# Grouping a split tile's wide products: all high halves first, then all low halves

## Chip, cores and metric

The kernel runs on one core of a Trainium2 chip. The metric is the device time of one execution in microseconds (us), the median of several runs. The engines that matter are TensorE (PE, with its weight loads PEld), VectorE (DVE), ScalarE (ACT) and the DMA queue of SyncE (SP).

## What is computed

One layer of a streaming encoder, in float32, for 256 tokens of width 2048:

```
h = modulate(rms_norm(x), shift1, scale1)
x = x + 0.5 * gate1 * (silu(h @ w1) * (h @ w3)) @ w2            # SwiGLU, hidden width 5632
h = modulate(rms_norm(x), shift2, scale2);  u = h @ w_in        # one projection, cut into parts
y_conv = silu(layer_norm(causal_conv31(glu(u_conv)))) @ pw_w
y_ret  = (silu(g) * group_norm(retention(rotary(q), rotary(k), v))) @ w_o
x = x + gate2 * ((sigmoid(gc) * y_conv + sigmoid(gr) * y_ret) @ w_out)
h = modulate(rms_norm(x), shift3, scale3)
x = x + 0.5 * gate3 * (silu(h @ w1b) * (h @ w3b)) @ w2b
out = modulate(rms_norm(x), shift_f, scale_f)
```

The shifts, scales and gates are products of silu(c) with large matrices (`adaT` in the kernel).

## The kernel before

Channels lie on the 128 partitions (P), the 256 tokens (T) on the free axis; 2048 channels are ND = 16 tiles. A float32 product is made out of exact halves. Every operand is split into a high half in the type fp32r and a low half, the difference. The product is then high x high + high x low + low x high, and the product of the low halves is left out.

Weights come in loads of up to 128 x 2048 elements (1 MB) into one of four `raw` tiles, through the one SP queue (`raw_load`, L92). `prep` (L170) splits each load in two: for each half of its blocks ACT copies up to 128 x 1024 elements into a `hi` tile (L180), and DVE subtracts it from `raw` into a `lo` tile (L182). There are five buffers of each (`HI`, `LO`). `prep` returns one pair (hi, lo) of slices for every 128 x 128 block; with 16 blocks in a load, the first eight lie in one hi tile and the last eight in the next. With 14 blocks they are seven and seven.

Two ways of multiplying stand side by side. `mm3` (L190) makes the three products of 256 columns each, one after the other, into one accumulator; `gemm` (L196) calls it for all blocks. `wide` (L201) makes two products per block instead. The block's high half is multiplied with both halves of the activations, which lie side by side as 512 columns, into a whole bank of 512 (L205). The block's low half is then multiplied with the activations' high half, 256 columns, into the second half of the same bank (L207). The two halves of the bank are added later (`total`, or twice in `Stream.add`). Each of these products loads its own 128 x 128 weights first.

`wide` is used for most of the kernel: the hidden tiles and the second matrices of both SwiGLUs (`ffn`, L333), the gates, `w_o`, `w_pw` and `w_out`. In the second matrix of a SwiGLU the 44 hidden tiles come as 28 and 16 (`GROUPS`); the 28 are loaded as twice 14 blocks. `gemm` or `mm3` is used for the start of each sub-layer, for q, k and the convolution's tiles, for the last column tiles of a sub-layer, and inside the retention's heads. There `value` (L520) calls `mm3` with the roles exchanged: slices of h are the stationary operand, and 512 columns of split weights move.

After each load a tick (L145) issues so much other work: loads of `adaT` that DVE reduces (L102), taps of the convolution, norms. The program's order within each engine is written by a planner that simulates a timeline (`schedule_with_timeline_sim=True`).

Of the kernel before, what the change touches and what calls it, by code (L numbers as in the profile page):

```python
# [14 lines left out]
P = 128  # L15
T = 256
# [10 lines left out]
EPS = 1e-6  # L27

S0 = 6                      # pairs of column tiles worked on side by side, with K outermost
SETS = 4                    # sets of such pairs that the first sub-layer begins with,  # L30
KGROUPS = [3, 4, 4, 5]      # in runs of so many tiles of K
PACE = 0.5                  # units of modulation per load of weights, meanwhile
GROUPS = [28, 16]           # hidden tiles between two visits to x
RAW, HI, LO = 4, 5, 5       # buffers of weights: as loaded, high halves, low halves
# units of modulation, and taps of the convolution, per load of weights
ADA_FFN1, ADA_GATES, ADA_OUT, ADA_FFN2 = 0.7, 0.35, 0.65, 0.35
TAPS_HEADS, TAPS_GATES = 3.8, 3.2

# columns of vecs
V_N1, V_NM, V_N2, V_NF = 0, 16, 32, 48  # L40
# [12 lines left out]
def hybrid_layer(ctx, tc, xT, c, vecs, rope, decay, adaT, w13, w13s, w13t, mixs, w2g, w_ab, w_qk, w_v, w_g,  # L53
# [4 lines left out]
    PE = nc.tensor  # L58
# [16 lines left out]
    x = sb(keep, [P, ND, T], "x1", tag="x")  # L75
# [59 lines left out]

    # ---- work that runs beside the products: so much of it after each load of weights
    rate = {"ada": ADA_FFN1, "taps": 0.0}
# [32 lines left out]
    def prep(src, nk, w, ticks=True):  # L170
        """Loads nk blocks of w columns and splits them; block k -> (hi, lo)."""
        n = nk * w
        r = raw_load(src, n)
        hk = (nk + 1) // 2
        got = []
        for k0 in range(0, nk, hk):
            k1 = min(nk, k0 + hk)
            c0, c1 = k0 * w, k1 * w
            hi = wp.tile([P, 1024], F32R, name="hi", tag="hi", bufs=HI)
            A.copy(hi[:, :c1 - c0], r[:, c0:c1])  # L180
            lo = wp.tile([P, 1024], F32R, name="lo", tag="lo", bufs=LO)
            V.tensor_tensor(lo[:, :c1 - c0], r[:, c0:c1], hi[:, :c1 - c0].bitcast(F32), op=ALU.subtract)  # L182
            for k in range(k0, k1):
                b = slice((k - k0) * w, (k - k0 + 1) * w)
                got.append((hi[:, b], lo[:, b]))
        if ticks:
            tick()
        return got

    def mm3(o, st, mv, start, stop, skip=False):  # L190
        """o += st * mv of exact halves (high, low), without the product of the low ones."""
        PE.matmul(o, st[0], mv[0], start=start, stop=False, skip_group_check=skip)  # L192
        PE.matmul(o, st[0], mv[1], start=False, stop=False, skip_group_check=skip)  # L193
        PE.matmul(o, st[1], mv[0], start=False, stop=stop, skip_group_check=skip)  # L194
# [6 lines left out]
    def wide(o, w, mv):  # L201
        """As gemm, in two parts to be added: o[:, :T] and o[:, T:]; the high half of w stays for both of mv's."""
        n = len(w)
        for k in range(n):
            PE.matmul(o, w[k][0], mv[k].rearrange("p a t -> p (a t)"), start=k == 0, stop=False,  # L205
                      skip_group_check=True)
            PE.matmul(o[:, T:], w[k][1], mv[k][:, 0], start=False, stop=k == n - 1, skip_group_check=True)  # L207

    def product(whole, o, w, mv):
        """gemm where the result is waited for, wide elsewhere."""  # L210
        if whole:
            gemm(o[:, 0:T], w, mv)
        else:
            wide(o, w, mv)

    def total(t, ps):
        """The sums of two column tiles' parts."""
        A.copy(t, ps[:, :, T:])
        V.tensor_tensor(t, ps[:, :, 0:T], t, op=ALU.add)
        return t  # L220
# [6 lines left out]
    def table(f):  # L227
        """Has the table of f in place before it is waited for."""
        A.activation(idle, eps, f)

    def rstd_from(sums, n, name):
        """1/sqrt(sums/n + EPS) by the table, then one Newton step."""
        y = sb(keep, [P, T], name + "_y", tag="rs_y")
        w = sb(keep, [P, T], name + "_w", tag="rs_w")
        r = sb(keep, [P, T], name + "_r", tag="rs_r")
        A.activation(y, sums, AF.Abs_reciprocal_sqrt, bias=eps[:, 0:1], scale=1.0 / n)  # L236
        V.tensor_scalar(w, sums, -0.5 / n, -0.5 * EPS, op0=ALU.mult, op1=ALU.add)
        V.tensor_tensor(w, w, y, op=ALU.mult)
        V.tensor_tensor(w, w, y, op=ALU.mult)
        V.scalar_tensor_tensor(out=r, in0=w, scalar=1.5, in1=y, op0=ALU.add, op1=ALU.mult)  # L240
        return r

    def partition_sums(parts, name):
        """The sum of the parts over tiles and partitions, on all partitions."""
        ps = banks2(name)
        for i, p in enumerate(parts):
            PE.matmul(ps[:, 0, 0:T], ones, p, start=i == 0, stop=i == len(parts) - 1)  # L247
        return ps[:, 0, 0:T]
# [7 lines left out]
    def squares(pool, t, tag="sq", bufs=1):  # L256
        """Adds the squares of two tiles of x to ssq."""
        if t == 0:
            A.activation(ssq, x[:, 0:2], AF.Square)
        else:  # L260
            sq = sb(pool, [P, 2, T], "sq", tag=tag, bufs=bufs)
            A.activation(sq, x[:, t:t + 2], AF.Square)
            V.tensor_tensor(ssq, ssq, sq, op=ALU.add)  # L263

    class Stream:
        """x as a sub-layer's tiles come in: x += gate * y, and the sums of its squares."""

# [22 lines left out]
    def modulated(pool, dst, t, r, n, j, between=None, spare="s"):  # L290
        """Tile t of x * r * scale + shift, split into dst."""
        a = sb(pool, [P, T], "xr", tag="g", bufs=2)
        V.tensor_tensor(a, x[:, t], r, op=ALU.mult)
        if between:
            between()
        if t < 2:
            A.activation(dst[:, t, 0], a, AF.Identity, bias=mod[:, j, t:t + 1], scale=scale[:, n, t:t + 1])  # L297
            f = sb(pool, [P, T], "hf", tag=spare, bufs=2 if spare == "s" else 1)
            V.tensor_scalar(f, a, scale[:, n, t:t + 1], mod[:, j, t:t + 1], op0=ALU.mult, op1=ALU.add)
            V.tensor_tensor(dst[:, t, 1], f, dst[:, t, 0].bitcast(F32), op=ALU.subtract)  # L300
            return
        A.activation(a, a, AF.Identity, bias=mod[:, j, t:t + 1], scale=scale[:, n, t:t + 1])
        A.copy(dst[:, t, 0], a)
        V.tensor_tensor(dst[:, t, 1], a, dst[:, t, 0].bitcast(F32), op=ALU.subtract)
# [12 lines left out]
    def side_by_side(srcs, h, ks, banks, ticks=True):  # L317
        """2 * S0 column tiles at once, a tile of K at a time: products begin with the first of h."""
        for i, k in enumerate(ks):
            w = prep(srcs[k], 2 * S0, P, ticks)  # L320
            across(w, h[k], banks, i == 0, i == len(ks) - 1)

    # ---- a SwiGLU's hidden tile, and its half step
    def hidden(pool, s):
        """From the two projections, in s: the activation's product, split."""
        A.activation(s[:, 0], s[:, 0], AF.Silu)
# [6 lines left out]
    def ffn(pool, i, h, s, store):  # L333
        """s: hidden tiles there already."""
        f0 = 0
# [28 lines left out]

    # ---- first half step: products begin as soon as the first tile of its modulated input is there
    with tc.tile_pool(name="ffn1", bufs=1) as pool:
# [50 lines left out]

    # ---- mixer
    with tc.tile_pool(name="mix", bufs=1) as pool:
# [27 lines left out]
        def normal(dst, n, name, done):  # L447
            """dst = (dst - mean) / std over its n tiles' channels, a few loads apart; then done()."""
            a = sb(pool, [P, 2, T], name + "_a", tag="cs_a", bufs=1)
# [27 lines left out]
        def conv_out():  # L477
            """Swish of the convolution's normed output, split."""
            rate["ada"] = ADA_OUT
# [12 lines left out]
        with tc.tile_pool(name="mix1", bufs=1) as p1:  # L492
# [27 lines left out]
            def value(hd):  # L520
                """v, tokens on partitions."""
                ps = banks2("ps")
# [15 lines left out]
            def scores(hd, qk):  # L538
                """Decayed scores, keys on partitions."""
                (q_hi, q_lo), (k_hi, k_lo) = qk  # L540
# [58 lines left out]
        with tc.tile_pool(name="mix2", bufs=1) as p2:  # L599
# [4 lines left out]
            def gate(src, t, ps=None):  # L604
                """Two tiles of a gate's projection."""
                if ps is None:
# [69 lines left out]

    # ---- second half step, and the final norm
    with tc.tile_pool(name="ffn2", bufs=1) as pool:
# [25 lines left out]
def _blocks(w):  # L704
    """[K, N] -> [N / P, P, K]: for a tile of P columns, per row in a tile of K, its blocks [K / P, P]."""
    k, n = w.shape
# [83 lines left out]
```

## Time and profile before

| | |
|---|---|
| median of 3 runs | 2357.58 us (2356.71 to 2358.31) |
| profiled execution, span from its first to its last instruction | 2354.9 us |
| PE busy (matmuls) | 2312.9 us, 98% |
| PEld busy (weight loads) | 2075.2 us, 88% |
| DVE busy | 1853.4 us, 79% |
| ACT busy | 1119.6 us, 48% |
| read from HBM | 609.77 MB, 261 GB/s over the span |

The median is 2.7 us above the span of the profiled execution: what lies around the first and last instruction, together with the difference between executions. Busy time of PE is a union of pipelined instructions: a new matmul starts while the one before is still shown as running. How fast PE works is therefore read from the distance between starts, not from durations.

### The profile page before, as it was taken

How to read it: one execution, taken by the hardware profiler on the slowest of the kernel's cores; microseconds unless marked ns; L12 is line 12 of the kernel's file. 1: busy time of each engine (PE TensorE's matmuls, PEld its weight loads, DVE VectorE, ACT ScalarE, POOL GpSimd, SP SyncE). 2: the span in 40 equal slices, each digit the busy share in tenths (PEclk: the TensorE clock that was granted, in tenths of full speed). 3: DMA queues.
4: the chain of work that ended last, by engine and by line, in shares of the span. 5: the costliest groups of instructions: out<-in, count | busy, mean ns of one | idle time of the engine just before them, and what ended most of it. 6: DMA issues, size and time to landing. Idle time of an engine off the chain costs nothing.

```text
span 2354.9 us, 35696 instructions
## 1 busy us (share of the span) xinstructions
PE 2312.9 (98%) x14460; PEld 2075.2 (88%) x14460; DVE 1853.4 (79%) x2384; ACT 1119.6 (48%) x1469; POOL 0.2 (0%) x4
## 2 busy tenths in 40 slices
PE   6999999999999999999999999999999999999997
PEld 5999988888888899998888888889888888888886
DVE  7888887888888668888998888877767666766675
ACT  5544653334544543545544644445544443344443
POOL 0000000000000000000000000000000000000000
PEclk9999999999999999999999999999999999999999
DMA  8989688898989465545676788866776677777662
GB/s 334 337 301 320 207 288 313 314 330 327 345 312 334 169 211 184 174 161 197 239 262 234 263 311 302 337 246 237 271 265 249 245 250 257 260 259 263 237 239 83
DMA packets 92183, 616.28 MB, mean 262 GB/s; under 512 B 10225, under 2 KB 10481, under 8 KB 34673
## 3 DMA queue, kind: packets, MB, share of 16 engines
q1 hardware_dynamic: 90290, 609.81, 72.0%
q10 hardware_dynamic: 1728, 4.20, 0.5%
q8 instruction: 113, 1.85, 0.3%
q14 instruction: 52, 0.43, 0.1%
HBM read 609.77 MB, written 4.19 MB: 261 GB/s over the span
## 4 chain that ended last, share of the span: by engine, by line
PE 94%; DVE 2%; DMA 2%; ACT 1%; issue 1%; SPq 0%; DVEq 0%; ACTq 0%
PE ps L205 43%; PE ps L207 22%; PE ps L193 9%; PE ps L192 9%; PE ps L194 9%; DMA raw<-in_w 2%; DVE lo L182 1%; DVE raw L102 0%; ACT hi L180 0%; DVE f L692 0%; DMA x<-in_xT 0%; DVE ssq L263 0%; ACT L236 0%; PE gn_m L247 0%; PE gn_v L247 0%
## 5 line engine op out<-in xcount | busy, mean ns | idle before, releaser
L180 ACT CAST hi<-raw 128x1024 fp32r<-128x1024 f32 (+2 forms) x864 | 845.1, 987 | 1103.8 <-PE ps L205 492.8
L182 DVE TENSOR_TENSOR lo<-raw,hi 128x1024 fp32r<-128x1024 f32 (+2 forms) x864 | 981.0, 1143 | 444.2 <-ACT hi L180 442.2
L205 PE MATMUL ps<-h,hi 128*128 128x512 f32 x2624 | 925.2, 397 | 0.0
L207 PE MATMUL ps<-h,lo 128*128 128x256 f32 x2624 | 736.8, 281 | 0.7 <-DVE lo L182 0.7
L205 PEld LDWEIGHTS ps<-h,hi 128*128 128x128 f32 x2624 | 492.6, 188 | 119.4
L207 PEld LDWEIGHTS ps<-h,lo 128*128 128x128 f32 x2624 | 495.7, 189 | 1.7 <-DVE lo L182 1.6
L205 PE MATMUL ps<-s,hi 128*128 128x512 f32 x1344 | 474.8, 398 | 0.0
L192 PE MATMUL ps<-h,hi 128*128 128x256 f32 x1472 | 415.1, 285 | 13.6 <-ACT h L297 13.6
L193 PE MATMUL ps<-h,hi 128*128 128x256 f32 x1472 | 417.8, 285 | 5.0 <-DVE h L300 4.9
L194 PE MATMUL ps<-h,lo 128*128 128x256 f32 x1472 | 415.9, 284 | 0.0
L102 DVE CUSTOM_DVE_ANT_0 raw<-raw,cb,vec 128x2048 f32<-128x2048 f32 x176 | 412.9, 2346 | 1.2 <-DMA raw<-in_adaT 1.2
L207 PE MATMUL ps<-s,lo 128*128 128x256 f32 x1344 | 377.3, 281 | 0.7 <-DVE lo L182 0.6
L205 PEld LDWEIGHTS ps<-s,hi 128*128 128x128 f32 x1344 | 252.4, 188 | 62.7
L192 PEld LDWEIGHTS ps<-h,hi 128*128 128x128 f32 x1472 | 283.2, 193 | 15.1 <-ACT h L297 15.1
L193 PEld LDWEIGHTS ps<-h,hi 128*128 128x128 f32 x1472 | 284.5, 193 | 6.0 <-DVE h L300 5.6
L194 PEld LDWEIGHTS ps<-h,lo 128*128 128x128 f32 x1472 | 283.8, 193 | 0.0
L207 PEld LDWEIGHTS ps<-s,lo 128*128 128x128 f32 x1344 | 253.9, 189 | 1.5 <-DVE lo L182 1.3
L442 DVE SCALAR_TENSOR_TENSOR acc<-y,vec,acc 128x256 f32<-128x256 f32 x240 | 113.3, 480 | 2.1
L205 PE MATMUL ps<-r,hi 128*128 128x512 f32 x256 | 90.8, 397 | 0.0
L205 PE MATMUL ps<-mg,hi 128*128 128x512 f32 x224 | 79.2, 397 | 0.0
L207 PE MATMUL ps<-r,lo 128*128 128x256 f32 x256 | 72.1, 282 | 0.0
L275 DVE SCALAR_TENSOR_TENSOR x<-ps,half_g,x 128x256 f32<-128x256 f32 x124 | 56.8, 479 | 16.8 <-PE ps L194 9.3
(171 smaller groups left out, 1562.5 us busy)
## 6 DMA issues: line engine op xcount, KB each, us to landing
raw<-in_adaT SPq DMA_DIRECT2D x176, 1024.0 KB, 5.9
raw<-in_w SPq DMA_DIRECT2D x148, 1024.0 KB, 5.3
raw<-in_w SPq DMA_DIRECT2D x64, 896.0 KB, 5.7
raw<-in_w13s SPq DMA_DIRECT2D x64, 768.0 KB, 6.0
raw<-in_w_v SPq DMA_DIRECT2D x16, 1024.0 KB, 4.9
raw<-in_w_g SPq DMA_DIRECT2D x16, 1024.0 KB, 4.9
raw<-in_w_gr SPq DMA_DIRECT2D x16, 1024.0 KB, 5.1
raw<-in_w_o SPq DMA_DIRECT2D x16, 1024.0 KB, 5.0
```

The lines of the kernel that those rows point to most:

```text
L102: tc.keep_in_program_order(V.tensor_tensor_reduce(r, r, cb, 1.0, vec[:, b:b + 1], op0=ALU.mult, op1=ALU.add, accum_out=mod[:, j, t:t + 1]))
L180: A.copy(hi[:, :c1 - c0], r[:, c0:c1])
L182: V.tensor_tensor(lo[:, :c1 - c0], r[:, c0:c1], hi[:, :c1 - c0].bitcast(F32), op=ALU.subtract)
L192: PE.matmul(o, st[0], mv[0], start=start, stop=False, skip_group_check=skip)
L193: PE.matmul(o, st[0], mv[1], start=False, stop=False, skip_group_check=skip)
L194: PE.matmul(o, st[1], mv[0], start=False, stop=stop, skip_group_check=skip)
L205: PE.matmul(o, w[k][0], mv[k].rearrange("p a t -> p (a t)"), start=k == 0, stop=False, skip_group_check=True)
L207: PE.matmul(o[:, T:], w[k][1], mv[k][:, 0], start=False, stop=k == n - 1, skip_group_check=True)
L275: V.scalar_tensor_tensor(out=x[:, t + u], in0=ps[:, u, part], scalar=self.gate[:, t + u:t + u + 1], in1=x[:, t + u], op0=ALU.mult, op1=ALU ...
L442: tc.keep_in_program_order(V.scalar_tensor_tensor(out=acc[:, t], in0=y[:, t, k:k + T], scalar=vec[:, dw + k:dw + k + 1], in1=acc[:, t], op ...
```

## The change

`prep` returns the hi tile too, as a mark of which blocks lie together. `wide` takes the blocks of one hi tile (eight, or seven in a load of 14) as a group: first all their products with the high halves, 512 columns each, then all their products with the low halves, 256 columns each. Number, shapes, operands and accumulators of the products stay as they were, and so do the loads and splits. Within a bank the order of the additions changes. The diff also takes comments out, which is left out here.

```diff
-                got.append((hi[:, b], lo[:, b]))
+                got.append((hi[:, b], lo[:, b], hi))
...
     def wide(o, w, mv):
         n = len(w)
-        for k in range(n):
-            PE.matmul(o, w[k][0], mv[k].rearrange("p a t -> p (a t)"), start=k == 0, stop=False,
-                      skip_group_check=True)
-            PE.matmul(o[:, T:], w[k][1], mv[k][:, 0], start=False, stop=k == n - 1, skip_group_check=True)
+        k0 = 0
+        while k0 < n:
+            k1 = k0
+            while k1 < n and w[k1][2] is w[k0][2]:
+                k1 += 1
+            for k in range(k0, k1):
+                PE.matmul(o, w[k][0], mv[k].rearrange("p a t -> p (a t)"), start=k == 0, stop=False,
+                          skip_group_check=True)
+            for k in range(k0, k1):
+                PE.matmul(o[:, T:], w[k][1], mv[k][:, 0], start=False, stop=k == n - 1, skip_group_check=True)
+            k0 = k1
```

## Rows read from the trace of the kernel before

**Rows 1.** The page: busy time, TensorE's granted clock in 40 slices, the chain by line.

```profile
PE 2312.9 (98%) x14460; PEld 2075.2 (88%) x14460; DVE 1853.4 (79%) x2384; ACT 1119.6 (48%) x1469; POOL 0.2 (0%) x4
...
PEclk9999999999999999999999999999999999999999
...
PE ps L205 43%; PE ps L207 22%; PE ps L193 9%; PE ps L192 9%; PE ps L194 9%; DMA raw<-in_w 2%; DVE lo L182 1%; DVE raw L102 0%; ACT hi L180 0%; DVE f L692 0%; DMA x<-in_xT 0%; DVE ssq L263 0%; ACT L236 0%; PE gn_m L247 0%; PE gn_v L247 0%
```

**Rows 2.** Groups of PE by line and form: names, shapes, count, busy us, mean ns.

```profile
L205 PE MATMUL ps<-h,hi 128*128 128x512 f32 x2624 | 925.2, 397 | 0.0
...
L205 PE MATMUL ps<-s,hi 128*128 128x512 f32 x1344 | 474.8, 398 | 0.0
...
L205 PE MATMUL ps<-r,hi 128*128 128x512 f32 x256 | 90.8, 397 | 0.0
...
L205 PE MATMUL ps<-mg,hi 128*128 128x512 f32 x224 | 79.2, 397 | 0.0
...
L205 PE MATMUL ps<-z,hi 128*128 128x512 f32 x128 | 45.4, 397 | 0.0
```

**Rows 3.** Groups of ACT by line and form: the hi tiles of seven blocks.

```profile
L180 ACT CAST hi<-raw 128x896 fp32r<-128x896 f32 x128 | 118.0, 942 | 201.4 <-PE ps L205 99.3 <-DMA raw<-in_w 83.2 <-PE ps L207 15.4
```

**Rows 4.** Windows, line 205 alone: stretch, length, PE (count), PEld (count), clock, DMA, GB/s.

```profile
530.00:695.00 165.00, 165.00 (x476) 88.98 (x477) 1.00 0.88 330
...
1680.00:2255.00 575.00, 575.00 (x1628) 305.78 (x1628) 1.00 0.71 255
```

**Rows 5.** Timeline of PE inside `wide`: start us, duration us, line, operands.

```profile
1899.95 0.40 PE L205 MATMUL ps<-h,hi 128*128 128x512 f32 x1
1900.18 0.28 PE L207 MATMUL ps<-h,lo 128*128 128x256 f32 x1
...
1901.01 0.40 PE L205 MATMUL ps<-h,hi 128*128 128x512 f32 x1
```

**Rows 6.** Timeline of PE: twelve narrow products, then a run of 512 columns (`value`).

```profile
1008.26 0.28 PE L192 MATMUL ps<-p_hi,v_hi 128*128 128x256 f32 x1
...
1009.69 0.39 PE L193 MATMUL ps<-lo,h 128*128 128x512 f32 x1
...
1011.31 0.40 PE L194 MATMUL ps<-hi,h 128*128 128x512 f32 x1
1011.54 0.39 PE L192 MATMUL ps<-hi,h 128*128 128x512 f32 x1
```

**Rows 7.** Timeline of PE: the first `value`, its products 1, 9 and 27.

```profile
858.57 0.40 PE L192 MATMUL ps<-hi,h 128*128 128x512 f32 x1
...
860.41 0.39 PE L194 MATMUL ps<-hi,h 128*128 128x512 f32 x1
...
864.49 0.39 PE L194 MATMUL ps<-hi,h 128*128 128x512 f32 x1
```

**Rows 8.** Timeline of PE in a `gemm`: products 1 and 35 of a run.

```profile
904.82 0.28 PE L192 MATMUL ps<-h,hi 128*128 128x256 f32 x1
...
908.90 0.28 PE L193 MATMUL ps<-h,hi 128*128 128x256 f32 x1
```

**Rows 9.** Timeline of PE at two stalls, and the window around them (PE, PEld, DVE, ACT, POOL).

```profile
475.92 0.42 PE L205 MATMUL ps<-s,hi 128*128 128x512 f32 x1
476.96 0.39 PE L207 MATMUL ps<-s,lo 128*128 128x256 f32 x1 [0.62 <-DVE lo L182]
...
528.88 0.39 PE L205 MATMUL ps<-h,hi 128*128 128x512 f32 x1
529.78 0.39 PE L207 MATMUL ps<-h,lo 128*128 128x256 f32 x1 [0.51 <-DVE lo L182]
...
450.00:570.00 120.00, 118.65 (x673) 102.77 (x672) 99.71 (x119) 47.27 (x57) 0.00 (x0) 1.00 0.90 328
```

**Rows 10.** Waits of ACT and of the SP queue: us in total, times, longest.

```profile
ACT hi L180 <- PE ps L205: 492.8, 353, 2.3
...
SPq L94 <- DVE lo L182: 1409.9, 353, 12.7
```

## The prediction, made before the changed kernel ran

> **What bounds the kernel now.** I read the page first. PE is busy for 98% of the span at full granted clock, and 92% of the chain that ended last runs over five lines of matmuls, 65% over the two of `wide` [rows 1]. So the kernel is as long as PE's instruction stream, and since number and shapes of the products stay, only the distance between their starts can change it. The groups by form give the count: 2624 + 1344 + 256 + 224 + 128 = 4576 pairs of a 512 and a 256 column product [rows 2].
>
> The windows then give the price of a pair as it alternates now. From 1680 to 2255 us it is 575 us / 1628 = 353.2 ns; from 530 to 695 us the same code takes 165 us / 476 = 346.6 ns [rows 4]. Both levels hold for hundreds of pairs, at the same clock. The timeline splits the slower one: three pairs take 1.06 us, with 0.23 to 0.24 us from a wide product to its narrow one and 0.12 us back [rows 5]. I take 235 and 118 ns. The reader should see that the trace holds two speeds of one instruction sequence, so the spacing is not fixed by the columns alone.
>
> Next, runs of one width, which is what the change makes. In `gemm` 34 distances of 256 column products, each with its own weight load, take 4.08 us: 120.0 ns [rows 8]. In the first `value` 18 distances of 512 columns, also with a load each, take 4.08 us: 226.7 ns [rows 7]. Together 346.7 ns, the faster of the two levels. So alternation at 353.2 ns loses 6.5 ns per pair against long runs. But a run pays for settling: behind twelve narrow products the first eight distances of 512 columns take 1011.54 - 1009.69 = 1.85 us, 231 ns each instead of 226.7 [rows 6]. The twelve narrow ones before take 1009.69 - 1008.26 = 1.43 us, 119.2 ns each [rows 6].
>
> **The change, part by part.** It adds no instruction and removes none. It turns the pairs into runs of eight and eight, or seven and seven. There are 128 hi tiles of seven blocks [rows 3], so 128 groups of seven with 896 pairs; the other 3680 pairs make 460 groups of eight.
>
> *A group of eight, slow level.* Before: 8 x 353.2 = 2.826 us. After, by the nearest rows: 1.85 us for the wide run, 8 x 119.2 = 0.954 us for the narrow one, 2.804 us. Saved 22 ns. The 476 pairs at the fast level are 60 groups of eight [rows 4]; I count the other 400 as slow: 400 x 22 = 8.8 us.
>
> *A group of seven.* Before 7 x 353.2 = 2.472 us. After: 1011.31 - 1009.69 = 1.62 us [rows 6], plus 7 x 119.2 = 0.834, 2.454 us. Saved 18 ns, x 128 = 2.3 us.
>
> *A group of eight, fast level.* Before 8 x 346.6 = 2.773 us, after 2.804: lost 31 ns, x 60 = 1.9 us.
>
> Sum of the spacing: 8.8 + 2.3 - 1.9 = 9.2 us gained. The bounds of the settling: nothing below, when transitions are as clean as in the fast level. A pair is then 346.7 ns, which gives 400 x 52 + 128 x 45.5 = 26.6 us. The first `value` lies between: 860.41 - 858.57 = 1.84 us for eight [rows 7], 10 ns per group better than I take, 5.9 us more over 588 groups. I take rows 6, because only there does a wide run follow a short narrow run that itself follows a wide one, as will be everywhere. Above, the wide products keep their 235 ns; that is the rival on the other side.
>
> A page of the Trainium skill speaks against grouping. "TensorE: Matmul & The Clock Gate", section "LDWEIGHTS (loading the stationary operand)", gives a load of 128 columns as 128/1.2, some 107 ns; 256 columns at 2.4 GHz are 107 ns too, so by this a run of narrow products leaves its loads no slack, while a wide product covers one twice over. The trace's run of narrow products at 120.0 against about 118 ns behind a wide one [rows 5, 8] fits a small price of that kind, 2 ns per product; it is already inside the sum.
>
> *The wait for lo.* Today each group needs its lo tile 0.23 us after its hi tile; after the change eight wide products later, 1.85 us. In the stretch with DMA at 90% [rows 9] some groups meet a lo that isn't there. At 475.92 the distance to the narrow product is 1.04 us instead of 0.235, at 528.88 it is 0.90: 0.80 + 0.66 = 1.5 us, with some shorter stalls beside. All of these lie within 1.6 us of new cover. I take 2 us, between 0 (the stretch is set by its loads, and what PE wins it waits for at the next hi tile) and 2.5 us.
>
> *Buffers.* The hi tile comes free at the end of the wide run, 0.95 us sooner; lo comes free when it did. ACT waits 353 times for a product of L205 to give back hi, 492.8 us in all, and SP waits for DVE's lo to give back raw, 1409.9 us [rows 10]. Both go earlier, or stay. This costs nothing and, with PE as the bound, wins nothing beyond the 2 us; the cover is SP's own long waiting. The next group's first hi tile is wanted about when it was, since a whole group takes as long within 1%. No semaphore, queue or DMA is added in front of anything.
>
> Total: 9.2 + 2 = 11.2 us. The profiled execution goes from 2354.9 to 2343.7 us; the median stands 2.7 us above the span, so **2346.4 us**.
>
> **Rivals.**
> *Clean transitions.* Groups settle at once, as the pairs from 530 to 695 us do [rows 4]. Then 26.6 + 2 = 28.6 us are gained: 2329 us. For it: that level exists and holds for 476 pairs. Against it: behind a change of width rows 6 and 7 both show some distances above 226.7.
>
> *The order does not matter.* What is lost sits in each product or in a state that the core falls into anyway, as it falls into two levels now [rows 4]; the grouped runs end within 4.7 us of before, at 2353 to 2362 us, say 2357. The same page's section "Back-to-back issue gap" gives this: start to start is N/2.4 + 2.5 ns, by the columns alone, so 325 ns per pair in any order. The trace disagrees, with 353.2 and 346.6 ns for the same columns [rows 4], so I hold this for less likely than a gain.
>
> *The wide product is slow by itself (the other side).* The runs of rows 6 and 7 have weights as the moving and h as the stationary operand; in `wide` it is the other way round, and no row shows 512 columns of h in a run. If such a product costs its 235 ns behind any neighbour, and the narrow one rises from 118 to 120, a pair takes 355 ns: 4100 x 1.8 + 476 x 8.4 = 11.4 us lost, less the 2 us of lo, so 2367 us. The point of decision: with narrow products at 119.2, the pairs' present 4100 x 353.2 + 476 x 346.6 = 1613 us are reached at 233.3 ns per wide product in the run; I forecast 231. Below it the change gains, above it loses. For it: the margin is 2 ns. Against it: with h moving, the 256 column products of `gemm` run at the clean 120.0 [rows 8], and 120 = 106.7 + 13.3 as 226.7 = 213.3 + 13.3: the same surplus over the columns for both widths and both roles.
>
> **How the numbers follow.** The forecast's own range runs from 2340 (the settling of rows 7) to 2352 us (nothing from lo, and half of the spacing): 0.50. Clean transitions, or nearly: 0.18. No matter: 0.17. Slow wide product: 0.15. 0.2% is 4.7 us, about what a measurement of this kernel can tell from no change; faster therefore means below 2352.9: 0.50 + 0.18 = 0.68. Same 0.17, slower 0.15. The range takes in clean transitions at the lower end, 2329, and most of the no-change case at the upper, 2361; the slow rival stays outside.
>
> **What would show it.** Right: in the timeline of `wide` eight starts of L205 about 231 ns apart, falling towards 227 within the run, then eight of L207 at 118 to 120; windows of 1680 to 2255 us with about 350.5 ns per pair; the stalls for lo at L207 gone; the fast level from 530 to 695 us gone as well. Wrong: L205 at 235 or more to the end of the run (the rival), or at 227 from its second product (clean). What would spoil it from outside is an order by the planner that breaks the runs up, seen as L205 and L207 still alternating, or new waits of PE for hi.

## The result, and the profile after

The changed kernel takes 2339.2 us (median of 4 runs, 2337.47 to 2340.9) against 2357.9 us for the kernel before (the median of 4 runs here): a ratio of 0.9925, with a 95% interval of 0.9911 to 0.9939. It is faster by 18.7 us; 11.2 us were forecast, and the time lies in the forecast's range, 0.8 us below the lower end (2340 us) of its narrower one. The profiled execution went from 2354.9 to 2336.1 us, 18.8 us.

The page of the changed kernel answers to [rows 1]: busy time, and the chain by engine and by line. L211 and L214 are now the wide and the narrow product of `wide`.

```profile
span 2336.1 us, 35687 instructions
...
PE 2296.1 (98%) x14460; PEld 2076.8 (89%) x14460; DVE 1851.7 (79%) x2384; ACT 1121.4 (48%) x1469; POOL 0.2 (0%) x4
...
PE 97%; DVE 1%; ACT 1%; issue 0%; DMA 0%; SPq 0%; DVEq 0%; ACTq 0%
PE ps L211 45%; PE ps L214 23%; PE ps L193 9%; PE ps L192 9%; PE ps L194 9%; DVE raw L102 0%; DVE lo L182 0%; DVE f L700 0%; DVE ssq L271 0%; DMA x<-in_xT 0%; ACT L244 0%; PE gn_m L255 0%; PE gn_v L255 0%; PE r L255 0%; DVE xr L301 0%
```

The same 14460 products fill 98% of a shorter span. The chain now runs through no load of weights: `DMA raw<-in_w` held 2% of it before and has gone, and `DVE lo L182` is down from 1%.

The timeline of PE in the changed kernel, one line for a run of equal products (start us, duration us, line, operands, count):

```profile
541.10 2.00 PE L211 MATMUL ps<-h,hi 128*128 128x512 f32 x8
...
680.76 2.00 PE L211 MATMUL ps<-h,hi 128*128 128x512 f32 x8
...
1542.02 2.02 PE L211 MATMUL ps<-mg,hi 128*128 128x512 f32 x8
1543.88 1.07 PE L214 MATMUL ps<-mg,lo 128*128 128x256 f32 x8
1544.79 2.02 PE L211 MATMUL ps<-mg,hi 128*128 128x512 f32 x8
...
1702.67 2.00 PE L211 MATMUL ps<-h,hi 128*128 128x512 f32 x8
1704.51 1.12 PE L214 MATMUL ps<-h,lo 128*128 128x256 f32 x8
1705.46 2.00 PE L211 MATMUL ps<-h,hi 128*128 128x512 f32 x8
...
1900.30 1.78 PE L211 MATMUL ps<-s,hi 128*128 128x512 f32 x7
1901.92 0.99 PE L214 MATMUL ps<-s,lo 128*128 128x256 f32 x7
1902.75 1.78 PE L211 MATMUL ps<-s,hi 128*128 128x512 f32 x7
```

Read starts, not durations. A group of eight with h takes 1.84 us for the wide run and 0.95 for the narrow one. Over 50 groups it is (680.76 - 541.10) / 50 = 2.793 us, 349.2 ns a pair. A group of seven takes 2.45 us. A group with mg takes 2.77 us: less, for the same shapes. Its wide run is longer, at 1.86 us, and its narrow one shorter, at 0.91; over all 224 pairs with mg the starts in the trace give 346.7 ns a pair. Of before, [rows 4] had 353.2 and 346.6 ns.

The stretch of the stalls, as in the last line of [rows 9], and what line 214 waited for:

```profile
450.00:570.00 120.00, 120.00 (x689) 105.53 (x688) 100.66 (x120) 49.10 (x60) 0.00 (x0) 1.00 0.91 329
```

```profile
L214 PE MATMUL ps<-z,lo x128: 276/281/286, 1362.8 to 1483.7; 128*128 128x256 f32 x128
its engine sat idle before it (us, times) until:
who waited for it (us, times):
```

PE is busy for all 120.00 us instead of 118.65, at 91% instead of 90% of the DMAs, and no narrow product finds its lo missing any more: the list of what ended the idle time is empty.

### The profile page after: what moved, and what is told of

It reads as the page before. It is cut to its first block, busy times and chain, and to the rows that moved or that the text cites. A ratio compares the mean times of both kernels' runs of the same rounds, so it can differ in the third digit from the quotient of the medians.

```text
span 2336.1 us, 35687 instructions
## 1 busy us (share of the span) xinstructions
PE 2296.1 (98%) x14460; PEld 2076.8 (89%) x14460; DVE 1851.7 (79%) x2384; ACT 1121.4 (48%) x1469; POOL 0.2 (0%) x4
## 4 chain that ended last, share of the span: by engine, by line
PE 97%; DVE 1%; ACT 1%; issue 0%; DMA 0%; SPq 0%; DVEq 0%; ACTq 0%
PE ps L211 45%; PE ps L214 23%; PE ps L193 9%; PE ps L192 9%; PE ps L194 9%; DVE raw L102 0%; DVE lo L182 0%; DVE f L700 0%; DVE ssq L271 0%; DMA x<-in_xT 0%; ACT L244 0%; PE gn_m L255 0%; PE gn_v L255 0%; PE r L255 0%; DVE xr L301 0%
## 5 line engine op out<-in xcount | busy, mean ns | idle before, releaser
L182 DVE TENSOR_TENSOR lo<-raw,hi 128x1024 fp32r<-128x1024 f32 (+2 forms) x864 | 982.2, 1144 | 413.6 <-ACT hi L180 409.5
L211 PE MATMUL ps<-h,hi 128*128 128x512 f32 x2624 | 658.0, 392 | 0.0
L211 PEld LDWEIGHTS ps<-h,hi 128*128 128x128 f32 x2624 | 471.8, 189 | 84.2
L194 PE MATMUL ps<-h,lo 128*128 128x256 f32 x1472 | 416.1, 284 | 0.0
L102 DVE CUSTOM_DVE_ANT_0 raw<-raw,cb,vec 128x2048 f32<-128x2048 f32 x176 | 413.1, 2347 | 1.1 <-DMA raw<-in_adaT 1.0
L214 PEld LDWEIGHTS ps<-h,lo 128*128 128x128 f32 x2624 | 357.9, 190 | 25.5
L214 PE MATMUL ps<-h,lo 128*128 128x256 f32 x2624 | 365.8, 282 | 0.0
L211 PE MATMUL ps<-s,hi 128*128 128x512 f32 x1344 | 339.5, 392 | 0.0
L192 PEld LDWEIGHTS ps<-h,hi 128*128 128x128 f32 x1472 | 283.5, 194 | 15.1 <-ACT h L305 15.1
L193 PEld LDWEIGHTS ps<-h,hi 128*128 128x128 f32 x1472 | 284.9, 194 | 5.9 <-DVE h L308 5.4
L194 PEld LDWEIGHTS ps<-h,lo 128*128 128x128 f32 x1472 | 284.2, 194 | 0.0
L211 PEld LDWEIGHTS ps<-s,hi 128*128 128x128 f32 x1344 | 240.9, 189 | 42.3
L214 PEld LDWEIGHTS ps<-s,lo 128*128 128x128 f32 x1344 | 185.5, 190 | 14.3
L214 PE MATMUL ps<-s,lo 128*128 128x256 f32 x1344 | 189.9, 282 | 0.0
L211 PE MATMUL ps<-r,hi 128*128 128x512 f32 x256 | 65.2, 396 | 0.0
L211 PE MATMUL ps<-mg,hi 128*128 128x512 f32 x224 | 56.7, 395 | 0.0
L211 PEld LDWEIGHTS ps<-r,hi 128*128 128x128 f32 x256 | 45.9, 188 | 8.7
```

Of the source, the lines that this page charges most:

```text
L102: tc.keep_in_program_order(V.tensor_tensor_reduce(r, r, cb, 1.0, vec[:, b:b + 1], op0=ALU.mult, op1=ALU.add, accum_out=mod[:, j, t:t + 1]))
```

## The experiments

Two theories of the gain were set against each other first: *settling* (a change of width costs some of the time of the new run, so fewer changes are cheaper) and *cover* (a group wants its lo tile later, so late lo tiles no longer stop PE). *Levels* was a third: short patterns fall into a level of their own, as the alternating one does.

### The low half lags, the order stays

```diff
     def wide(o, w, mv):
         n = len(w)
+        for k in range(n + 4):
+            if k < n:
+                PE.matmul(o, w[k][0], mv[k].rearrange("p a t -> p (a t)"), start=k == 0, ...)
+            if k >= 4:
+                PE.matmul(o[:, T:], w[k - 4][1], mv[k - 4][:, 0], start=False, ...)
```

> Alternation kept, but each low half comes four wide products later: wide 0 to 3, then narrow k and wide k+4 in turn, then the last four narrow ones. lo is wanted 0.93 us later than hi, more than the longest stall of 0.80 us, so this gives the cover almost without the grouping. Settling: the alternating part (three quarters) keeps its 352.5 ns on the mean, the rest gains some 3 us, the stalls go (2.6 us): 2352 us. Cover: nearly the whole 18.7 us, 2340 us. Levels: as settling where the alternation stays at 353 ns, or 2329 us where it falls to 346.7.

Measured: 2354.62 us, ratio 0.9989 (0.998 to 0.9998). Windows of this kernel, first all engines, then line 205 alone:

```profile
450.00:570.00 120.00, 120.00 (x683) 104.28 (x682) 102.12 (x122) 50.91 (x62) 0.00 (x0) 1.00 0.91 337
...
1680.00:2240.00 560.00, 522.35 (x1590) 292.59 (x1589) 1.00 0.72 255
```

The stalls have gone, as in the changed kernel, while a pair still takes 560 us / 1590 = 352.2 ns. The profiled execution is 2352.5 us, 2.4 us below before; the interval of the ratio allows 0.5 to 4.7 us. So cover is worth about 2.4 of the 18.8 us, and most of the rest is spacing.

The starts in the traces split it more sharply. Take the distances behind the products of `wide`, and set apart what those above 300 ns have beyond a usual one (230 or 118 ns). The distances then add up to 1613.1 us before, 1612.4 us with the lagging order and 1596.9 us in the changed kernel; what was set apart is 2.9, 0.8 and 0.8 us. By this 16.2 us are spacing and 2.1 us cover.

### Runs of other lengths

Runs of two and of four cut the groups of the changed kernel:

```diff
-            while k1 < n and w[k1][2] is w[k0][2]:
+            while k1 < n and k1 - k0 < 2 and w[k1][2] is w[k0][2]:     # or 4
```

A whole load makes runs of sixteen (fourteen), by another mark in `prep` (and a bound of sixteen in `wide`, which is not shown):

```diff
-                got.append((hi[:, b], lo[:, b], hi))
+                got.append((hi[:, b], lo[:, b], r))
```

The snake turns every second group round, so that runs are sixteen long while each tile is held for one group only:

```diff
+            for low in (False, True) if first else (True, False):
+                for k in range(k0, k1):
+                    ...   # the narrow product if low, else the wide one
+            first = not first
```

> Runs of two: two wide products, two narrow ones, and so on. Theory 'settling' (each change of width costs some excess over 226.7 and 120.0 ns, paid by the first five or so products of the new run): per two pairs the first two distances of the settled changed kernel, 233 and 236, then about 114 and 119, so about 701 ns or 350.5 ns a pair; spacing gains 9 us, half of the lo stalls go (1.3 us), 2347 us. Rival 'levels' (short periods fall into one of the two levels of the kernel before whatever the order, and only long runs escape): 353.2 ns a pair and 2356 us, or 346.7 ns a pair and 2329 us. Rival 'cover' (the gain came from lo being wanted later, not from the spacing): cover 0.46 us of the 1.85, so at most a third of the 18.7 us, 2352 us or more, with the pair at 353 ns outside the stretch with busy DMAs.

> Runs of four. Settling: four wide distances at 233, 236, 228, 227 and four narrow ones at 114, 119, 120, 120 give 1397 ns, about 349.3 ns a pair; spacing gains 14 us and the lo stalls go (cover 0.93 us against a longest stall of 0.80), 2342 us, between runs of two and runs of eight. Levels: 353.2 or 346.7 ns a pair in long stretches, so 2353 or 2329 us. Cover: most of the stalls' part is there already, so the same time as runs of eight, 2339 us, with the pair still near 353 ns where the DMAs are not busy.

> Runs of a whole load: sixteen wide products over two hi tiles, then sixteen narrow ones (fourteen in the loads of fourteen). Settling: one change of width back and forth per load instead of two, which saves 20 ns per load of the changed kernel's 5586: 286 loads, less those of r, mg and z that settle otherwise, some 5 us, 2334 us. Levels: nothing further, 2339 us, since runs of eight already escape. Rival on the other side, 'buffers': the first lo tile of a load is held 1.9 us longer, so with five lo tiles DVE splits later, PE waits for lo or hi in the stretches with busy DMAs, and the time is 2340 us or more, with new idle time of PE behind DVE lo L182 or ACT hi L180 from 310 to 700 us.

> The changed kernel with every second group turned round: high, low, then low, high, so that runs are sixteen long inside a load while hi and lo tiles are held no longer than for a group of eight. Theory 'settling' for runs of eight and more (20 ns per change of width back and forth, whatever the length of the run): half of the changes go, about 250 x 20 ns, 5 us, 2334 us. Rival 'late lo': the second group's lo tile is wanted first, 0.95 us sooner than in the changed kernel, so stalls come back and it ends at 2339 us or more.

| order | median us | ratio, 95% interval |
|---|---|---|
| runs of two | 2337.92 | 0.9918, 0.9904 to 0.9931 |
| runs of four | 2345.32 | 0.9951, 0.9938 to 0.9963 |
| the change: runs of eight or seven | 2339.2 | 0.9925, 0.9911 to 0.9939 |
| whole load: sixteen or fourteen | 2337.36 | 0.9918, 0.9905 to 0.9932 |
| snake: sixteen or fourteen | 2335.99 | 0.991, 0.9898 to 0.9923 |

Timelines of PE for the runs of two, of four, of a whole load and of the snake, all with h:

```profile
1700.36 0.63 PE L209 MATMUL ps<-h,hi 128*128 128x512 f32 x2
...
1702.45 0.62 PE L209 MATMUL ps<-h,hi 128*128 128x512 f32 x2
```

```profile
475.35 1.20 PE L209 MATMUL ps<-s,hi 128*128 128x512 f32 x4 [1.38 <-ACT hi L180]
...
1701.43 1.09 PE L209 MATMUL ps<-h,hi 128*128 128x512 f32 x4
...
1704.24 0.63 PE L209 MATMUL ps<-h,hi 128*128 128x512 f32 x2
```

```profile
1492.37 1.22 PE L209 MATMUL ps<-mg,hi 128*128 128x512 f32 x2 [3.80 <-DVE mg L620]
...
1704.20 3.82 PE L209 MATMUL ps<-h,hi 128*128 128x512 f32 x16
...
1709.76 3.59 PE L209 MATMUL ps<-h,hi 128*128 128x512 f32 x15
```

```profile
1690.78 3.82 PE L215 MATMUL ps<-h,hi 128*128 128x512 f32 x16
...
1701.91 2.46 PE L215 MATMUL ps<-h,hi 128*128 128x512 f32 x10
```

Against the clean 346.7 ns a pair, three groups of two take 2.09 us, so 0.697 us each, 4 ns too many. Two groups of four take 2.81 us, 1.405 each, 18 too many. A group of eight at 2.793 is 20 over, and one of sixteen (5.56 for the whole load, 11.13 / 2 for the snake) is 13 to 18 over at this resolution; the median of all with h is 5.567 us in both traces, 20 over. For eight and sixteen the excess per change back and forth is the same, whatever the length. Settling holds there: the snake came out 2 us from its figure, although its interval overlaps that of the change, and the distances behind its products of `wide`, added up as above, are 4.6 us less than the change's, where 5 were forecast. For short runs it failed: settling expected a group of two at 701 ns and the kernel at 2347 us; the group took 697 ns and the kernel 2337.92 us, level with runs of eight. Runs of four missed too, with 1405 ns a group for 1397 and 2345.32 us for 2342. So the sizes do not follow one law of settling; short patterns have levels of their own, and what sets these stays open.

The whole load is no faster than the change, though its pairs are closer. Its waits show one that the changed kernel hardly has (0.8 us in all), DVE waiting for PE to give back lo:

```profile
DVE lo L182 <- PE ps L212: 202.4, 145, 3.5
```

The stall that costs most is elsewhere: 3.80 us for mg in the timeline above. ACT's cast of mg came behind a split that itself waited for its load. Whether this comes of tiles that are held longer, or of the order that the planner wrote anew, is not shown, nor is it for the 1.38 us for hi in the runs of four.

### Where the tiles lie

Groups of mg (and of r, in the same buffer) took 2.77 us in the changed kernel, 2.79 with h and s. The sizes of the kernel's tiles, added up in the order of its pools, put h, s2 and the split weights at distances from each other that are multiples of 128 bytes in each partition. r and mg start 178880 bytes behind h, an odd multiple of 64. Pads of 64 bytes tell whether that is the cause; a second pad behind the moved tile keeps all others on their places modulo 128:

```diff
+    sb(keep, [P, 16], "shift")
     crow = sb(keep, [1, D], "crow", tag="h")     # h takes this buffer later
+    sb(keep, [P, 16], "shift2")
```

The same pad in front of the pools of the two SwiGLUs moves s2, one in `wp` moves the weights (with further pads that put back the tiles behind them), and 8 columns instead of 16 move h by 32 bytes.

> The changed kernel with the tile h moved by 64 bytes, from a multiple of 128 to an odd multiple of 64, where r, mg lie; all else stays on its place modulo 128. Theory 'place' (where the moving tile lies modulo 128 bytes decides how PE's stream settles): the groups of h fall from 2793 to the 2773 ns that mg's have in the changed kernel, 328 groups, 6.6 us, 2333 us; and if the narrow products of mm3 with h run at the 113.3 ns at which mg's 96 do, instead of 120.0, some 4400 x 6.7 = 29 us more, 2303 us. Rival 'history' (the cleaner level of r and mg is a phase that an earlier event in that stretch leaves behind): h stays at 2793 and 120 ns, 2339 us.

> The kernel before with the same move of h, alternation kept. Place: the alternating pairs of h take on the pattern of r and mg in the kernel before (235 and 118 ns all along, no level of 346.6), 353.2 ns on the mean; narrow products of mm3 with h at mg's 117.7 ns instead of 120.0 gain some 10 us: 2347 us; the grouping is what lets the place pay, so far less than e5 gains. If alternation alone was the fault of place, its pairs would fall to 346.7 everywhere: 2327 us. History: no change, 2357 us.

> As e5, and the hidden tiles s2 moved by 64 bytes as well. Place: the 180 groups of s gain 20 ns each (3.6 us) and 192 narrow products of mm3 6.7 ns each (1.3 us), so 5 us below e5. History: no difference from e5 beyond noise.

> The changed kernel with the split weights (raw, hi, lo) moved by 64 bytes and h, s, r, mg where they were modulo 128. Theory 'moving tile' (only the place of the moving tile counts): groups of h at 2793, of mg at 2773, narrow products of h at 120.0, so 2339 us. Rival 'both' (what counts is whether the moving and the stationary tile lie alike modulo 128): h and s, now unlike the weights, take on the levels of e7 (2773 and 113 to 118 ns), r and mg, now alike, go to 2793: 2312 to 2316 us.

> e7 with the split weights moved by 64 bytes too, so h, s, r, mg and weights all lie at an odd multiple of 64. Moving tile: as e7, 2312 us. Both: h, s, r, mg now alike with the weights, all groups at 2793 and narrow products at 120.0, 2340 us.

> The changed kernel with h moved by 32 bytes instead of the 64 of e5. If halves of 128 bytes are what counts, 2339 us, with groups of h at 2793; if any place off 128 does it, 2319 us, with 2773; a third level would say that the place matters in finer steps.

> e7 with runs of two instead of eight. Settling: with h and s moved a change of width costs nothing in runs of eight (2773 ns, which is 346.7 a pair), so runs of two can't gain, and lose where a change costs again: 2312 us or a few more. Levels: runs of two have a level of their own, below 346.7 in the best case as s shows in e7 (2740 ns, 342.5 a pair), so 2305 us or less.

| kernel | moved | median us | ratio, 95% interval |
|---|---|---|---|
| changed | h by 64 | 2318.73 | 0.9832, 0.9816 to 0.9848 |
| before | h by 64 | 2337.39 | 0.9922, 0.9908 to 0.9937 |
| changed | h and s2 by 64 | 2311.54 | 0.9802, 0.9784 to 0.982 |
| changed | weights by 64 | 2306.48 | 0.9797, 0.9778 to 0.9816 |
| changed | h, s2 and weights by 64, modulo 128 | 2342.99 | 0.9938, 0.9926 to 0.9951 |
| changed | h by 32 | 2337.67 | 0.9917, 0.9904 to 0.9931 |
| runs of two | h and s2 by 64 | 2315.99 | 0.9818, 0.9802 to 0.9834 |

Timeline of PE with h moved:

```profile
1702.59 2.02 PE L213 MATMUL ps<-h,hi 128*128 128x512 f32 x8
1704.45 1.07 PE L216 MATMUL ps<-h,lo 128*128 128x256 f32 x8
1705.36 2.02 PE L213 MATMUL ps<-h,hi 128*128 128x512 f32 x8
...
1902.09 1.78 PE L213 MATMUL ps<-s,hi 128*128 128x512 f32 x7
...
1904.53 1.78 PE L213 MATMUL ps<-s,hi 128*128 128x512 f32 x7
```

Timeline of PE with the weights moved:

```profile
1510.54 2.00 PE L212 MATMUL ps<-mg,hi 128*128 128x512 f32 x8
1512.38 1.12 PE L215 MATMUL ps<-mg,lo 128*128 128x256 f32 x8
1513.33 2.00 PE L212 MATMUL ps<-mg,hi 128*128 128x512 f32 x8
...
1690.96 2.02 PE L212 MATMUL ps<-h,hi 128*128 128x512 f32 x8
1692.83 1.07 PE L215 MATMUL ps<-h,lo 128*128 128x256 f32 x8
1693.74 2.02 PE L212 MATMUL ps<-h,hi 128*128 128x512 f32 x8
...
1901.93 1.76 PE L212 MATMUL ps<-s,hi 128*128 128x512 f32 x7
...
1904.35 1.78 PE L212 MATMUL ps<-s,hi 128*128 128x512 f32 x7
```

Timeline of PE with h, s2 and the weights moved:

```profile
1701.63 2.02 PE L214 MATMUL ps<-h,hi 128*128 128x512 f32 x8
...
1704.43 2.03 PE L214 MATMUL ps<-h,hi 128*128 128x512 f32 x8
...
1900.79 1.78 PE L214 MATMUL ps<-s,hi 128*128 128x512 f32 x7
...
1903.23 1.78 PE L214 MATMUL ps<-s,hi 128*128 128x512 f32 x7
```

And windows with nothing but narrow products of `mm3` with h: the changed kernel, h moved (two windows), the weights moved, and the kernel before with h moved (two windows).

```profile
100.00:290.00 190.00, 190.00 (x1586) 190.00 (x1585) 165.32 (x226) 94.89 (x145) 0.00 (x0) 1.00 0.79 282
```

```profile
100.00:290.00 190.00, 190.00 (x1616) 1.00 0.80 286
1580.00:1630.00 50.00, 50.00 (x443) 1.00 0.83 294
```

```profile
100.00:290.00 190.00, 190.00 (x1679) 190.00 (x1678) 171.64 (x238) 99.09 (x150) 0.00 (x0) 1.00 0.82 297
```

```profile
100.00:290.00 190.00, 190.00 (x1679) 190.00 (x1678) 171.77 (x238) 98.36 (x149) 0.00 (x0) 1.00 0.81 296
```

```profile
870.00:925.00 55.00, 55.00 (x469) 1.00 0.54 190
```

With h moved, its groups go from 2.79 to 2.77 us, and s, which wasn't, stays at 2.44 to 2.45. With the weights moved instead, h gets the 2.77 to 2.78 and mg, which hadn't moved, loses it (2.79). So it is not the moving tile's place that counts, as *moving tile* had it, but its place relative to the weights: *both* was right, also in its harder forecast, that moving everything alike takes the gain back (2343 us). A group of seven with s takes 2.42 us with the weights moved, and 2.44 to 2.45 again where s moved along with them. For h that run is no clean test: its pads move h by 64 bytes and the weights by 192, so the distance changes by 128, and groups of h take 2.80 to 2.82 us.

From 100 to 290 us the narrow products go from 190 us / 1586 = 119.8 ns to 117.6 with h moved and 113.2 with the weights moved. That is where most of these gains lie: the kernel has some 4400 such products with h, and 4400 x 6.6 ns = 29 us for the weights moved. But the two paces are not one for each move. With h moved the same products take 50 us / 443 = 112.9 ns from 1580 to 1630 us of the same execution, and in the kernel before with h moved 113.2 from 100 to 290 us and 55 us / 469 = 117.3 from 870 to 925. So a distance off by 64 bytes allows two paces. In the traced execution with h moved the slower one held for most of these products, which accounts for much of what is missing to the 2303 us of *place*.

The kernel before with h moved still alternates at the slow pace (its line 207 takes 560 us / 1586 = 353.1 ns from 1680 to 2240 us), and grouping then gains 2337.39 - 2318.73 = 18.7 us, as much as without the move. The two gains add up, as far as the executions can tell, which scatter by 8 us in the kernel before with h moved and by 11 in the changed one. *If any place off 128 does it* fell: at 32 bytes groups of h take 2.80 us, as the next timeline shows, while the total is within the interval of the unmoved. Its narrow products did gain, to 190 us / 1621 = 117.2 ns from 100 to 290 us, so 32 bytes give a level of their own. Runs of two with the tiles moved are no faster than runs of eight, against *levels*.

```profile
1702.57 2.03 PE L213 MATMUL ps<-h,hi 128*128 128x512 f32 x8
...
1705.37 2.03 PE L213 MATMUL ps<-h,hi 128*128 128x512 f32 x8
```

The changed kernel with the weights moved has the lowest median: 2306.48 us, 2.0% below the kernel before. Its lead over the move of h and s2 is not shown: its executions run from 2303.61 to 2316.28 us, those from 2302.56 to 2315.07.

## Why the prediction was right

*PE's stream bounds the kernel, and only the spacing can change it.* Right: 16.2 of 18.8 us are spacing and 2.1 us waits, by the starts.

*A group of eight, slow level.* Right in kind, too small: 2.804 us forecast, 2.793 measured, so 33 ns saved instead of 22. The step that failed was the size of the settling, by the choice of its row. I took the run behind twelve narrow products [rows 6] for the nearest; the first `value` [rows 7], at 1.84 us for eight, has the size that came out, and the narrow run took 0.95. Whether that row was nearer for a reason, such as where its tiles lie, which I did not look at, no run tests. For 400 groups the step is worth 400 x 11 = 4.4 us.

*A group of seven.* 2.454 forecast, 2.45 us measured; at 349.2 ns a pair it would be 2.444.

*Fast level.* Those groups lost some 20 ns each, not 31: 0.7 us. That level did vanish from 530 to 695 us, as forecast.

*Not in the sum.* The groups of r and mg came out at 2.77 us, the time of the rival *clean transitions*, which had 0.18, but not by its mechanism: the wide run takes 1.86 us, 232.5 ns each, and the narrow one 0.91 us, some 114 ns each, where the rival had 226.7 and 120.0. They are 60 groups; about 1 us.

*The wait for lo.* 2 us taken; 2.4 us measured by the lagging order alone, 2.1 us by the starts. The stalls were gone from the windows, as the text asked to see.

*Sum again.* 400 x 33 ns + 128 x 25 ns - 60 x 20 ns + 1 us = 16.2 us, and 2.1 us of lo: 18.3 us of the 18.8 measured.

*Rivals.* The order does matter. The formula of the Trainium skill, "TensorE: Matmul & The Clock Gate", section "Back-to-back issue gap", by which the start to start goes by the columns alone, does not hold here: the same columns took 353, 349.2 and 346.7 ns a pair. The section gives that formula for the isolated gap and says that in a stream with weight loads both set the spacing, which the prediction left out. The wide product is not slow by itself: with h as moving operand the run of eight takes 1.84 us, 230 ns each, below the 233.3 ns of decision; the reversed operands of rows 6 and 7 did no harm. The total of clean transitions came out for r and mg, and for h after a move of 64 bytes, but with a slower wide run and a faster narrow one, and for a reason that was not among my cases.

*Buffers.* Nothing new waited for hi or lo in the changed kernel, as written; it did appear where lo is held longer (the whole load).

## What to carry to other kernels

Where one engine is busy for 98%, read the distance between starts of its instructions by kind of neighbour, over long stretches; two levels of one sequence mean that something besides the shapes sets the pace, and its difference times the count is a first size of what an order may win; here that was 27 us (4100 pairs x 6.6 ns), and the order won 16. Group products of one width where buffers allow it, and check what the order does to the waits: here it also let the low halves be wanted later, which ended a wait and was about an eighth of the gain. When choosing a row to price a sequence that the trace does not show, compare where the tiles lie too, not only the shapes; and try a pad of 64 bytes between moving and stationary tiles before any larger rewrite.

## What the runs showed of the hardware that was not expected

- The pace of a float32r product with its own weight load depends on where the moving tile lies relative to the weights. Narrow products (256 columns) take 119.8 ns where the distance is a multiple of 128 bytes, and 117.6 or 113.2 where it is off by 64, all at full granted clock.
- Both of these paces occur in one execution, for the same products: with h moved 117.6 ns from 100 to 290 us and 112.9 from 1580 to 1630. What chooses between them is open, so one trace of each kernel doesn't tell whether moving the weights is better than moving h and s2.
- A change of place can speed up narrow products and slow down wide ones: a run of eight wide products took 1.86 us with mg and 1.84 with h, the narrow run behind it 0.91 and 0.95.
- 128 bytes may not be the whole of it. With all three moved, s lies as far from the weights as before and its groups are back at 2.44 to 2.45 us, while h, 128 bytes farther from them, takes 2.80 to 2.82 for eight instead of 2.79. The runs do not say why.
- The excess of a change of width does not grow evenly with the run: 6.5 ns for runs of one, 4 for two, 18 for four, 20 for eight and for sixteen.
